# A gated linear attention decay in a four-branch decoder layer: other buffers, other place

## The chip, the cores and the metric

The kernel runs on one core of one Trainium2 chip. TensorE does the matrix products, VectorE, ScalarE and GpSimd the elementwise work, and SP (SyncE) issues all DMA transfers. The metric is the device time of one execution in microseconds (us), lower is better.

## The reference

One decoder layer over 2048 tokens of width 1024, all in float32. After an RMSNorm, one combined projection feeds four branches: A is RG-LRU, B an mLSTM, C is HGRN2, D is a gated linear attention (GLA). Each branch is gated by a SiLU path and projected, the four are merged by sigmoid gates, and one output projection, a residual and a last RMSNorm follow. C and D use the same chunked recurrence (chunks may be of another length, as long as the sums agree):

```python
log_gk = jax.nn.log_sigmoid(g_lr @ g_w_lr2 + g_b_lr2) / GLA_GATE_TAU      # tau 16, rank 16 -> 256 channels
og = gla_chunkwise(q, k, v, log_gk)
# gla_chunkwise, per chunk, with G the running sum of log_gk:
A = einsum(qc, kc, exp(G_t - G_s))            # s <= t
o = A @ vc + (qc * exp(G)) @ state
state = exp(G_last) * state + (kc * exp(G_last - G)).T @ vc
```

`g_lr` is the 16-wide, low-rank part of the combined projection. The decay `log_gk` of branch D is what the change is about.

## The kernel before, in words

The tokens are done in two halves of 1024. Each half goes through the same stages: the normalised input is split into a high and a low part (`hh`, `hl`, eight tiles each), because a float32 product is made of three products of rounded parts. Then most of the combined projection is done in pairs (`ahead_pairs`), its results going out to DRAM. Then come the mixers (`mixers`), the merge (`merge`) and the output projection (`outp`).

In `mixers` three things run beside each other. First, twelve tiles of 512 tokens, steps 0 to 11: steps 0 to 7 are HGRN2 heads, 8 to 11 are pairs of GLA heads. Each is one call of `gla_tile`. A tile clips the decay to a slot `g8` on GpSimd (L969), sums it up, forms the diagonal products (L993), then makes four sweeps over block sizes 8, 16, 32 and 64, each with its own temporary `w` (L1006) that GpSimd fills (L1012, L1013); at the end it transposes, scales by its gate (L1103) and sends the result to the array `y` in DRAM (L1106). Second, the mLSTM, whose pieces are traced between those of the tiles. Third, direct projections that fill TensorE: four value projections `ip_vals` (L280) and six late merge gates (`gates_ahead`, L268). Their weights are loaded by SP (L248), split by ScalarE (L249) and GpSimd (L250).

The last two value projections, at steps 4 and 6, also give 8 channels each of the low-rank input, which VectorE copies to `lrt` (L1125). `gla_decay` needs both. Per half it transposes `lrt` in two groups of four (L1168) and copies each group to a temporary `lt` (L1169); then, for two channel tiles and two token tiles, it multiplies by the 16-row weight `wlr` (L1175), adds the bias and applies Abs, Exp and Ln on ScalarE (L1177 to L1179 and, for Ln, the helper's L227) and ends with two operations on VectorE (L1181, L1182). Its four results are the decays of steps 8 to 11.

Temporaries come from an arena of 40 slots of 516 floats (the first 16 named `arena` in the trace, 8 `ma`, 16 `mb`). The arena hands out the next free slot in turn, at tracing time; what writes to a slot has to wait for the last use by the slot's owner before. PSUM has eight banks: two, `pb`, are taken in turn by the direct projections, six, `mx`, in turn by everything else in the mixers. A bank's or slot's users follow each other in the order in which they were traced.

The order of instructions on each engine is made by a list scheduler with its own timing model: what is ready goes by priority, and the priority is the place in the traced program, put forward by 4000 for the mixers (`mix`) and by 6000 for loads and evictions of projections. Engines run their queues in order. `lw` is a 128x1024 float tile that holds the LRU's weights earlier in each half and serves as a gate buffer in the merge. `merge` reads `y` back into `hh` and `hl` (L1291 to L1293), which it can only do when the direct projections have read these.

Of the kernel before, what the change touches and what calls it, by code (L numbers as in the profile page):

```python
# [8 lines left out]
F32 = mybir.dt.float32  # L9
# [6 lines left out]
P = 128  # L16
# [82 lines left out]
class Arena:  # L99


    def __init__(self, tile, n):
        self.where = [(tile, i) for i in range(n)]
        self.used = [False] * n
        self.live, self.at, self.peak = {}, {}, 0
        self.base, self.lim = 0, None
# [41 lines left out]
class Trunk:  # L148
    def __init__(self, ctx, tc, a, out, dbg=None):
        self.tc, self.nc, self.a, self.out, self.dbg = tc, tc.nc, a, out, dbg or {}  # L150
        nc = self.nc
        self.const = ctx.enter_context(tc.tile_pool(name="const", bufs=1))
        self.psum = ctx.enter_context(tc.tile_pool(name="psum", bufs=1, space=bass.MemoryType.PSUM))
        self.dram = ctx.enter_context(tc.tile_pool(name="dram", bufs=1, space=bass.MemoryType.DRAM))
        c = self.const
        self.hh = [c.tile([P, HT], F32R, name=f"hh{k}") for k in range(KT)]
        self.hl = [c.tile([P, HT], F32R, name=f"hl{k}") for k in range(KT)]
        self.wr = [c.tile([P, 528], F32, name=f"wr{k}") for k in range(3)]
        self.wh = [c.tile([P, 528], F32R, name=f"wh{k}") for k in range(NW)]
        self.wl = [c.tile([P, 528], F32R, name=f"wl{k}") for k in range(NW)]  # L160
        self.wi = self.gt = 0
        self.gth = [c.tile([P, 512], F32, name=f"gth{k}") for k in range(2)]
        self.ar = Arena(c.tile([P, NU * U], F32, name="arena"), NU)
        self.pb = [self.psum.tile([P, 512], F32, name=f"pb{i}") for i in range(NPB)]
        self.bi = 0
        self.tanhs, self.table = [], None
        self.mx = [self.psum.tile([P, 512], F32, name=f"mx{i}") for i in range(8 - NPB)]
        self.mi = 0
        self.ydram = [self.dram.tile([4, P, HT], F32, name=f"y{n}") for n in range(4)]
        self.gdram = [self.dram.tile([P, HT], F32, name=f"g{j}") for j in range(32)]  # L170
        self.pdram = {n: self.dram.tile([w, P, HT], F32, name=f"p{n}") for n, w in PRE + (("xm", 4), ("hf", 4), ("hg", 4))}
        self.mdram = [self.dram.tile([8, P, HT], F32, name=f"m{n}") for n in range(2)]
        self.adram = [self.dram.tile([P, 512], F32, name=f"a{k}") for k in range(4)]
        self.rdram = [self.dram.tile([2, 4, 512], F32, name=f"rdram{i}") for i in range(2)]
# [984 lines left out]
    def gla_decay(self):  # L1159

        nc = self.nc
        V, A, T = nc.vector, nc.scalar, nc.tensor
        gs = []
        lt = self.F()
        for n in range(2):
            ps = self.bank()
            for c in range(4):
                T.transpose(ps[0:16, c * 128:(c + 1) * 128], self.lrt[:, n * 4 + c, :], self.cs("id"))  # L1168
            V.tensor_copy(lt[0:16, n * 512:(n + 1) * 512], ps[0:16])  # L1169
        for p in range(2):  # L1170
            gs.append([self.T(0, NU + 2 * NA if p else None) for _ in range(2)])
            for n in range(2):
                g, t = gs[p][n], self.T()
                ps = self.bank()
                T.matmul(ps, self.wlr[:, p * 128:(p + 1) * 128], lt[0:16, n * 512:(n + 1) * 512], start=True, stop=True)  # L1175
                gg, tt = g[:, :512], t[:, :512]
                A.activation(gg, ps, AF.Identity, bias=self.pv("gb", p))  # L1177
                A.activation(tt, gg, AF.Abs)
                A.activation(tt, tt, AF.Exp, scale=-1.0)  # L1179
                self.ln(tt, tt, bias=1.0)  # L1180
                V.scalar_tensor_tensor(gg, gg, 0.0, tt, op0=ALU.min, op1=ALU.subtract)  # L1181
                V.tensor_scalar(gg, gg, 1.0 / 16, None, op0=ALU.mult)  # L1182
                self.free(t)
        self.free(lt)
        return gs


    def mixers(self):
        mix = lambda: self.prio(self.MIX)
        self.ahead = 0  # L1190
        low = NU + 2 * NA
        fill = iter(FILL)
        self.gates_ahead(next(fill))
        other = self.mlstm()
        due = 0.0

        def both(gen):

            nonlocal due
            for _ in iter(lambda: next(gen, 1), 1):  # L1200
                due += RATE
                while due >= 1:
                    due -= 1
                    next(other, None)

        with mix():
            for _ in range(LEAD):
                next(other, None)
        hv = self.ip_vals(0, 256)
        steps = [(j, gi) for j in range(6) for gi in range(2)]  # L1210
        gv, gd, loads = [], [], {}

        def load(s):
            j, gi = steps[s]
            if s >= LIM:
                self.ar.base, self.ar.lim = NTH, low
            if j < 4:
                loads[s] = [self.load_p(n, j, gi) for n in ("hq", "hf", "hg")], [self.load_p("hz", j, gi)]
            else:
                loads[s] = ([self.load_p(n, j - 4, gi) for n in ("gq", "gk")],  # L1220
                            [self.load_p("gz", 2 * j - 8 + i, gi) for i in range(2)])

        load(0)
        for s, (j, gi) in enumerate(steps):
            if s == 1:
                hv += self.ip_vals(1, 256)
            elif s == 4:
                gv += self.ip_vals(2, 264, self.lrt[:, :, 0:8])
            elif s == 6:
                self.ar.lim = low  # L1230
                gv += self.ip_vals(3, 264, self.lrt[:, :, 8:16])
                self.ar.lim = None
            elif s == 7:
                with mix():
                    gd = self.gla_decay()
            if s + 1 < len(steps):
                load(s + 1)
            self.gates_ahead(next(fill))
            x, zs = loads.pop(s)
            with mix():  # L1240
                if j < 4:
                    both(self.gla_tile(2, gi, [j], *x, [hv[j][gi]], zs, [(0, 128)], self.S[j], self.eps_h))
                else:
                    p = j - 4
                    both(self.gla_tile(3, gi, [2 * p, 2 * p + 1], *x, gd[p][gi], [v[gi] for v in gv[2 * p:2 * p + 2]], zs,
                                       [(0, 64), (64, 64)], self.S[j], self.eps_g))
        with mix():
            for _ in other:
                pass
        self.ar.base, self.ar.lim = 0, None  # L1250
# [298 lines left out]
```

## Time and profile before

| | |
|---|---|
| median of 3 runs | 2726.04 us (2724.26 to 2729.91) |
| the profiled execution | 2737.6 us |
| its span, first to last instruction | 2735.8 us |
| mean granted TensorE clock, as a share of 2.4 GHz | 0.977 |
| mixers, first half | about 740 to 1200 us, the last part beside the merge |
| mixers, second half | about 2100 to 2550 us, the last part beside the merge |
| decay, first half | 978.8 us (first transpose) to 1019 us |
| decay, second half | 2327.7 us to 2371 us |

A profile comes from one execution, so sums are made against its own time. In the rows, a busy share is an engine's share of the stretch, PEclk the granted clock as a share of full speed, and the text in brackets at the end of a timeline row says how long the engine sat idle before the instruction and which instruction's end released it. A matmul of float32 operands is recorded as two instructions.

### The profile page before, as it was taken

Reading aid. Unit: us, or ns where it says so; the run is one execution under the profiler, and the core shown is the slowest. Engines: PE = TensorE matmul, PEld = TensorE weight load, DVE = VectorE, ACT = ScalarE, POOL = GpSimd, SP = SyncE. Lnnn points to the kernel's source line nnn. Section 1 sums busy time; section 2 is a strip of 40 time slices with the busy share of each in tenths; the row PEclk is TensorE's granted clock in tenths of the full one; section 3 lists DMA queues with packets and bytes.
Section 4 is the critical chain, followed back from the end, with each engine's and each line's share of the span. In section 5 each row is a group of like instructions: output and inputs, shape, how many; then the busy total and the mean of one; then the engine's idle time right before and its main releaser. Section 6 shows DMA issues by size and latency. Waiting matters only on the chain. (4 is left out here: it accounts for less than half of the span.)

```text
span 2735.8 us, 45795 instructions
## 1 busy us (share of the span) xinstructions
PE 2604.2 (95%) x16800; PEld 2155.0 (79%) x16800; DVE 1739.0 (64%) x2907; ACT 1296.8 (47%) x2769; POOL 1500.4 (55%) x1273
## 2 busy tenths in 40 slices
PE   7999999999998898999999999999999999999999
PEld 5777878878788886778977777788787888776789
DVE  8787676447667778634376957754657667775332
ACT  5455444434444464452454454454345455644533
POOL 5566556444555555466475566554445555654753
PEclk9999999999999998999999999999999989999999
DMA  6233223443454336785442432243346433558721
GB/s 227 70 127 104 85 85 131 135 135 112 156 178 126 103 123 205 271 288 160 140 139 77 140 115 85 89 131 124 123 131 203 129 106 120 183 168 289 260 95 74
DMA packets 227073, 393.03 MB, mean 144 GB/s; under 512 B 20721, under 2 KB 78081, under 8 KB 226849
## 3 DMA queue, kind: packets, MB, share of 16 engines
q1 hardware_dynamic: 226848, 390.11, 43.2%
q8 instruction: 132, 2.16, 0.3%
q14 instruction: 93, 0.75, 0.1%
HBM read 270.42 MB, written 119.60 MB: 143 GB/s over the span
## 5 line engine op out<-in xcount | busy, mean ns | idle before, releaser
L418 POOL TENSOR_TENSOR wl<-wr,wh 128x512 fp32r<-128x512 f32 x264 | 370.2, 1407 | 300.5 <-ACT wh L417 292.2
L418 POOL TENSOR_TENSOR wl<-gth,wh 128x512 fp32r<-128x512 f32 x198 | 286.4, 1447 | 280.7 <-ACT wh L417 266.7
L423 PE MATMUL mx<-s,wh 128*128 128x512 f32 x1248 | 395.0, 396 | 5.5 <-DVE arena L432 2.4
L432 DVE TENSOR_TENSOR arena<-arena,mx 128x512 f32<-128x512 f32 x386 | 252.8, 681 | 184.4 <-PE mx L423 168.1
L250 POOL TENSOR_TENSOR wl<-wr,wh 128x512 fp32r<-128x512 f32 (+1 forms) x176 | 248.5, 1420 | 194.1 <-ACT wh L249 159.3
L423 PE MATMUL mx<-hh,wl 128*128 128x512 f32 x824 | 328.1, 398 | 9.4 <-POOL wl L418 9.4
L423 PE MATMUL mx<-hh,wh 128*128 128x512 f32 x824 | 326.8, 397 | 5.8 <-DVE mqk L624 3.6
L423 PE MATMUL mx<-hl,wh 128*128 128x512 f32 x824 | 327.5, 397 | 2.4 <-DVE hl L306 2.3
L268 PE MATMUL pb<-hh,wh 128*128 128x512 f32 x704 | 291.0, 415 | 11.4 <-DVE lw L1319 4.0
L268 PE MATMUL pb<-hl,wh 128*128 128x512 f32 x704 | 287.6, 409 | 3.2 <-DVE hl L1293 3.2
L268 PE MATMUL pb<-hh,wl 128*128 128x512 f32 x704 | 286.5, 407 | 0.0
L423 PEld LDWEIGHTS mx<-s,wh 128*128 128x128 f32 x1248 | 235.7, 189 | 62.7 <-DVE arena L432 2.8
L417 ACT ACTIVATE wh<-wr 128x512 fp32r<-128x512 f32 x264 | 164.2, 627 | 229.0 <-PE mx L423 142.6
L280 PE MATMUL pb<-wh,hh 128*128 128x256 f32 (+1 forms) x880 | 254.2, 290 | 3.6 <-DVE lrt L1125 2.3
L280 PE MATMUL pb<-wl,hh 128*128 128x256 f32 (+1 forms) x880 | 253.9, 289 | 1.7 <-POOL wl L250 1.7
L280 PE MATMUL pb<-wh,hl 128*128 128x256 f32 (+1 forms) x880 | 253.5, 288 | 0.0
L423 PE MATMUL mx<-s,wl 128*128 128x512 f32 x624 | 245.5, 397 | 0.0
L417 ACT ACTIVATE wh<-gth 128x512 fp32r<-128x512 f32 x198 | 124.3, 628 | 228.5 <-DVE gth L428 184.4
L423 PEld LDWEIGHTS mx<-hh,wl 128*128 128x128 f32 x824 | 155.8, 189 | 51.5 <-POOL wl L418 16.0
L423 PEld LDWEIGHTS mx<-hh,wh 128*128 128x128 f32 x824 | 156.4, 190 | 46.3 <-issue 7.0
L249 ACT ACTIVATE wh<-wr 128x512 fp32r<-128x512 f32 (+1 forms) x176 | 110.2, 629 | 165.0 <-PE pb L268 110.1
L423 PEld LDWEIGHTS mx<-hl,wh 128*128 128x128 f32 x824 | 155.9, 189 | 41.1 <-DVE hl L306 3.6
(614 smaller groups left out, 6081.8 us busy)
## 6 DMA issues: line engine op xcount, KB each, us to landing
wr<-in_wc_dram SPq DMA_DIRECT2D x246, 256.0 KB, 2.7
g<-arena SPq DMA_DIRECT2D x52, 512.0 KB, 3.4
gth<-in_wc_dram SPq DMA_DIRECT2D x66, 256.0 KB, 2.8
wr<-in_wb_dram SPq DMA_DIRECT2D x64, 256.0 KB, 3.3
hl<-y SPq DMA_DIRECT2D x32, 512.0 KB, 5.9
arena<-g SPq DMA_DIRECT2D x48, 256.0 KB, 4.5
arena<-in_xT_dram SPq DMA_DIRECT2D x32, 256.0 KB, 5.2
lw<-g SPq DMA_DIRECT2D x32, 256.0 KB, 3.6
```

Source lines behind the costliest of these rows:

```text
L249: nc.scalar.activation(hi, raw, AF.Copy)
L250: nc.gpsimd.tensor_tensor(lo, raw, hi, op=ALU.subtract)
L268: nc.tensor.matmul(ps, w[:, ws], h[:, ts], start=(k == 0 and i == 0), stop=(k == nk - 1 and i == 2))
L280: self.nc.tensor.matmul(v, h[:, cs], w[:, ws], start=(first and i == 0), stop=(last and i == 2))
L417: A.activation(hi, w, AF.Copy)
L418: G.tensor_tensor(lo, w, hi, op=ALU.subtract)
L423: nc.tensor.matmul(ps, wp[:, ws], xp, start=(k == 0 and i == 0), stop=(k == 3 and i == 2))
L432: V.tensor_tensor(o, x, y, op=ALU.add)
```

## The change

The transposed low-rank input goes to `lw` and no longer to an arena pair. The elementwise temporary of the four rounds is one tile of its own, `dt`, and no longer a new arena slot for each. The transposes and the 16-row matmuls take their banks from the direct projections' two, and no longer from the six others. The call stands in step 6, right behind the last value projection and ahead of that step's loads and tile, and no longer in step 7. To make room for `dt`, the scratch memory for DMA descriptors is made smaller. The rotation of both sets of banks is the same after the call as before, as six uses are a multiple of two and of six.

```diff
+        self.dt = c.tile([P, 512], F32, name="dt")
...
-        lt = self.F()
+        lt = self.lw.rearrange("p a b -> p (a b)")
         for n in range(2):
-            ps = self.bank()
+            ps = self.pbank()
...
-                g, t = gs[p][n], self.T()
-                ps = self.bank()
+                g = gs[p][n]
+                ps = self.pbank()
...
-                gg, tt = g[:, :512], t[:, :512]
+                gg, tt = g[:, :512], self.dt
...
-                self.free(t)
-        self.free(lt)
...
                 gv += self.ip_vals(3, 264, self.lrt[:, :, 8:16])
                 self.ar.lim = None
-            elif s == 7:
                 with mix():
                     gd = self.gla_decay()
...
-    nc = bacc.Bacc("TRN2", target_bir_lowering=False, num_devices=1)
+    nc = bacc.Bacc("TRN2", target_bir_lowering=False, num_devices=1, dynamic_dma_scratch_size=1024)
```

## Rows read from the trace of the kernel before

**Rows 1.** The page, busy time of each engine over the span.
```profile
PE 2604.2 (95%) x16800; PEld 2155.0 (79%) x16800; DVE 1739.0 (64%) x2907; ACT 1296.8 (47%) x2769; POOL 1500.4 (55%) x1273
```
**Rows 2.** The chain of waits, its longest piece: start, us, engine, tile, line.
```profile
2551.89 73.10 PE pb L268 x315
```
**Rows 3.** Table by stretches: busy PE, PEld, DVE, ACT, POOL; PEclk; DMA share; GB/s.
```profile
1000.00:1012.00 12.00, 12.00 (x77) 8.53 (x76) 5.73 (x14) 8.23 (x15) 4.58 (x6) 0.86 0.66 219
1028.00:1060.00 32.00, 24.09 (x324) 18.52 (x321) 31.49 (x52) 17.45 (x35) 16.62 (x17) 0.84 0.70 244
1084.00:1096.00 12.00, 11.08 (x134) 8.93 (x135) 9.18 (x21) 2.99 (x6) 5.56 (x6) 0.57 0.57 185
1084.00:1200.00 116.00, 109.94 (x1061) 84.77 (x1062) 62.40 (x118) 53.74 (x144) 51.48 (x52) 0.96 0.79 273
2352.00:2360.00 8.00, 8.00 (x42) 4.83 (x36) 3.46 (x7) 6.26 (x12) 2.80 (x4) 0.79 0.66 199
2376.00:2404.00 28.00, 21.82 (x256) 17.53 (x255) 27.47 (x43) 16.15 (x33) 16.23 (x14) 0.82 0.82 282
2425.00:2552.00 127.00, 118.72 (x1152) 90.47 (x1151) 66.48 (x125) 60.21 (x154) 57.61 (x56) 0.95 0.75 256
```
**Rows 4.** Timeline of GpSimd, first half: sweeps of step 7, then step 8.
```profile
1001.16 0.62 POOL L1012 TENSOR_TENSOR arena<-mb 128x256 f32<-128x256 f32 x1 [0.63 <-DVE mb L1181]
...
1017.13 1.41 POOL L1012 TENSOR_TENSOR arena<-mb 128x256 f32<-128x256 f32 x1 [2.68 <-DVE arena L1181]
1021.05 0.80 POOL L1012 TENSOR_TENSOR arena<-mb 128x256 f32<-128x256 f32 x1
...
1034.55 1.51 POOL L1012 TENSOR_TENSOR arena<-mb 128x256 f32<-128x256 f32 x1 [2.52 <-DVE mb L968]
...
1042.11 0.79 POOL L1012 TENSOR_TENSOR arena<-mb 128x256 f32<-128x256 f32 x1
```
**Rows 5.** Timeline of VectorE, first half: two of the decay's four L1181.
```profile
1000.09 0.99 DVE L1181 SCALAR_TENSOR_TENSOR mb<-mb,arena 128x512 f32<-128x512 f32 x1
...
1016.37 0.68 DVE L1181 SCALAR_TENSOR_TENSOR arena<-arena 128x512 f32<-128x512 f32 x1
```
**Rows 6.** Timeline of GpSimd, second half: first and last sweep of step 7.
```profile
2350.45 0.86 POOL L1012 TENSOR_TENSOR arena<-mb 128x256 f32<-128x256 f32 x1 [0.63 <-DVE mb L1181]
...
2372.43 0.61 POOL L1012 TENSOR_TENSOR arena<-mb 128x256 f32<-128x256 f32 x1
```
**Rows 7.** The decay's lines over both halves: ns min/median/max, first and last start.
```profile
L1168 PE MATMUL mx<-cst,lrt x16: 270/272/277, 978.8 to 2346.8; 128*16 128x128 f32 x16
L1175 PE MATMUL mx<-mb,wlr x16: 587/588/891, 991.7 to 2358.2; 16*128 16x512 f32 x16
L1169 DVE COPY mb<-mx x4: 667/670/678, 982.7 to 2350.3; 16x512 f32<-16x512 f32 x4
L1177 ACT ACTIVATE arena<-mx,pvt x6: 669/682/687, 1004.1 to 2358.8; 128x512 f32<-128x512 f32 x6
```
**Rows 8.** Timelines of SP and GpSimd: `y` transfer of step 6, clip of step 7.
```profile
1001.71 0.32 SPq L1106 DMA_DIRECT2D y<-arena  x1
...
978.20 1.49 POOL L969 TENSOR_SCALAR mb<-arena 128x512 f32<-128x512 f32 x1 [2.35 <-issue]
```
**Rows 9.** Timelines of VectorE and TensorE around the end of the value projections.
```profile
986.66 0.16 DVE L1125 COPY lrt<-pb 128x8 f32<-128x8 f32 x1
...
989.44 0.47 PE L268 MATMUL pb<-hh,wh 128*128 128x512 f32 x1
...
995.84 0.27 PE L1168 MATMUL mx<-cst,lrt 128*16 128x128 f32 x1
...
999.42 0.68 DVE L1169 COPY mb<-mx 16x512 f32<-16x512 f32 x1
...
1002.95 1.98 PE L1175 MATMUL mx<-mb,wlr 16*128 16x512 f32 x4
```
**Rows 10.** Table by stretches, only instructions on the direct projections' banks.
```profile
989.00:1004.00 15.00, 11.08 (x43) 7.13 (x41) 0.36 (x2) 0.86 (x2) 1.00 0.67 223
```

## The prediction

> **What bounds the kernel now.** I read the page's busy line first: TensorE is busy for 95% of the span, VectorE for 64%, GpSimd for 55% [rows 1]. The chain of waits ends in one unbroken run of projection matmuls on TensorE; its longest piece lasts 73.10 us [rows 2]. So time can only come from two places: from moments when TensorE has nothing to do, and from moments when its clock is granted at less than full speed. The change removes no matmul. I therefore went to the table by stretches and looked at TensorE's busy time and clock in the mixers and in the merge that follows, where the decay's results are used.
>
> The stretch in which the decay runs loses little: TensorE is busy for all 12 us from 1000, with the clock granted at 0.86. The loss comes after it, where the last direct projections have run out and the merge cannot yet go at full rate. From 1028 to 1060 TensorE is busy for 24.09 of 32 us at a clock of 0.84: 7.9 us idle and, at 0.16 of 32, 5.1 us of clock, 13.0 together. In the second half the same place (2376 to 2404) loses 6.2 and 5.0, which is 11.2. VectorE is what is full there, 31.49 of 32 and 27.47 of 28. The tail in which GLA tiles run beside the merge loses 6.1 + 4.6 and 8.3 + 6.4, together 25.4 us in 243 [rows 3]. The changed code can touch these 24.2 and 25.4 us, not the 2604 of work.
>
> The timeline of GpSimd shows what the decay does to the mixers now. In step 7 (the eighth tile) the first operation of the four sweeps, L1012, starts at 1001.16, and at 1021.05 for the last: 19.9 us for four sweeps. Two of them are released by L1181 of the decay. In the next tile, with no decay about, the same four take 1034.55 to 1042.11, 7.6 us [rows 4]. VectorE's L1181 rows fit: one ends at 1001.08, one at 1017.05, and the sweeps follow 0.08 us later [rows 5]. The code says why: the decay's four temporaries `t` and the four sweep temporaries `w` get the same arena slots, one after the other. In the second half the four sweeps take 2350.45 to 2372.43, 22.0 us [rows 6]. So tile 7 is held by up to 12.3 and 14.4 us per half.
>
> **The change, part by part.**
>
> Work: nothing is added or removed. Per half there are still 8 transposes of 0.27 us, 8 matmul records of 0.588 us (two to a matmul), two copies of 0.67 us, four Identities of 0.68 us and their followers [rows 7]. The decay issues no DMA and nothing on GpSimd, so no transfer moves with it; it is traced ahead of the loads for step 7 and of tile 6, but passes nothing of SP's or GpSimd's queue except by the slots that it takes. The smaller DMA scratch costs nothing: every DMA listed on the page is issued by SP. `lw` is next written by the merge's gate loads, which come tens of microseconds later; cost nothing.
>
> Temporary `dt`: tile 7's sweeps no longer wait for L1181, a gain of up to 12.3 and 14.4 us of lead for the mixers. What is late next? I followed the slots by hand. With four decay outputs taken before tile 6 and no `t`, tile 7's clipped decay (L969) falls on the slot of tile 6's gate, which must first go out to `y`; that transfer is issued at 1001.71, while L969 now starts at 978.20 [rows 8]. From 1002 the front of tile 7 needs seven instructions of 0.7 to 1.5 us by the nearest rows, about 7 us, so its sweeps can be joined at 1009 at the earliest instead of 1021. I take a lead of 8 us per half, two thirds of the upper end; the lower end is none.
>
> What the lead is worth: nothing at its own place, where TensorE is full, but VectorE has 12 - 5.73 = 6.3 us free there (8 - 3.46 = 4.5 in the second half) which it lacks in the full stretch [rows 3]. If that much mixer work moves forward, the full stretch shortens by as much, at its own loss of 13.0/32 = 0.41 and 11.2/28 = 0.40 per us: 2.6 + 1.8 = 4.4 us. The tail shortens by the 8 us of lead twice: 16 of 243 us, with 25.4 us lost in them, 1.7 us. Ends: none, and all the 24.2 us of the two full stretches.
>
> One `dt` for four rounds makes the next Abs wait for the last L1181. Behind it on ScalarE stand weight splits and evictions, for which GpSimd's L250 and then the projections wait. By rows a round is three activations and one L1181, about 2.6 us, so four take some 10 us. That ends near 1002 (now the last L1181 starts past 1016 [rows 5]), and its first user, tile 8, starts later; cost nothing. If that cover fails, the four rounds' 10 us fall on tile 8.
>
> Bank pair `pb`: the next gate's first matmul is queued behind the decay's last use of its bank, with the mixers' matmuls behind it on TensorE and the gate's eviction, and later the merge, waiting for it. The chain starts when the last but one value group has been copied (986.66 + 0.16): four transposes 1.1, copy 0.67, matmul 1.18, Identity 0.68, matmul 1.18, Identity 0.68: 5.5 us, ending at 992.3. The gate now starts at 989.44 [rows 9], so it is 2.9 us late at best. Of 15 us there, instructions on `pb` take 11.08, 74% of TensorE [rows 10], so 2.1 us would be idle; but two of the decay's matmuls (2.4 us), which now displace projections, lie in the hole. I take 0.5 us per half, 1.0 in all. The upper end: the copy now starts 3.3 us after the transpose before it has ended (996.11 to 999.42 [rows 9]); three such delays, one for the copy and one for each Identity, make the hole 12.8 us, 9.5 us idle per half.
>
> Clock: four records of the 16-row matmul stand together at 1002.95 (1.98 us [rows 9]), and around them the clock is granted at a mean between its 1.2 and 2.4 GHz levels although TensorE counts as busy: 0.14 of 12 us, 1.7 us, and 0.21 of 8, 1.7 us, in the second half [rows 3]. On two banks with an Identity between they can't stand together. I take half of the 3.4 as gained, 1.7. Ends: 3.4 gained, or a new fall of the size of 1084 to 1096, 0.43 of 12, 5.2 us per half [rows 3].
>
> Here the Trainium skill speaks against the change. In TensorE: Matmul & The Clock Gate (section "A second HAM failure mode: psum-queue depth-cycling") it says that a kernel which walks through PSUM banks in each iteration leaves TensorE idle for short moments so often that its clock falls back and forth. By that rule two banks for six uses would bring a new fall instead of ending one, and the sum would be on the slow side; the stretch from 1084 shows that the clock can be at 0.57 with TensorE busy for 11.08 of 12 us [rows 3].
>
> **Sum.** Against the profiled execution of 2737.6 us (span 2735.8 and 1.8 around it): -4.4 - 1.7 - 1.7 + 1.0 = -6.8, so 2730.8. The median of the runs shown is 2726.04, 0.99578 of that; the forecast on that scale is 2719.3 us, 0.25% faster.
>
> **Rivals.**
>
> No change: the lead is real and worth nothing, because TensorE's work is fixed and the merge's own copies of `y` through VectorE set the full stretch. For it: TensorE's 95%; and tile 7's new wait for the `y` transfer may eat the lead. Against it: VectorE is full exactly there. Time: 2737.6 - 1.7 + 1.0 = 2736.9, or 2725.3. If the change doesn't do what it says (the stall moves from the sweeps to L969), this is also the time.
>
> Slower: the two-bank chain starves TensorE behind the last value projection. For it: in-order queues on VectorE and ScalarE that delayed the decay's copy by 3.3 us; the projections have no other bank. Against it: the mixers' matmuls and the decay's own fill a quarter of the hole and more. With two delays the hole is 2.9 + 6.6 = 9.5 us, 7.0 idle per half, 14.0 in all; with the lead's 6.1 kept, +7.9: 2745.5, or 2733.9. With one fall of the clock, 5.2 more: 2739.1. It decides once more than 3.9 us per half are idle there, half of the 7.8 gained elsewhere.
>
> Much faster: both full stretches lose their idle time and their low clock: -24.2 - 1.7 + 1.0, or 2701. For it: VectorE's 100% there; against it, ten us of lead can't empty a stretch of 32.
>
> **How the numbers follow.** A measurement of this kernel can tell about 0.2%, 5.5 us, from no change. Forecast 0.40 (its own range 2712 to 2720), much faster 0.06, no change 0.28, slower 0.26. So faster 0.46, same 0.28, slower 0.26. The range runs from 2704, a third of the way from the far case's 2701 to the forecast's own low end, to 2737, most of the slow case.
>
> **What would show it.** Right: tile 7's four L1012 within some 8 to 12 us and none released by L1181; the 16-row matmuls apart; TensorE's idle time in the full stretches down from 7.9 and 6.2 us by 2 to 3 each. The gate's first matmul at most 3 us behind the last value matmul. L969 of tile 7 released by the `y` transfer shows my slot reading right. Wrong: more than 4 us of TensorE idle between the last value projection and the next gate, waiting on an L1177 or the copy; a clock under 0.8 there; or sweeps that are fast while the full stretches lose the same 24 us.

## The result: 1.2% slower, and the profile after

The changed kernel takes 2760.46 us in the median of 4 runs (2756.88 to 2761.73), the kernel before 2726.82 in the median of 4 (2724.26 to 2729.91): a ratio of 1.0121, 95% interval 1.0103 to 1.0138. The profiled execution took 2761.7 us with a span of 2759.9 us and a mean granted clock of 0.975. The forecast was 2719.3 us, the range 2704 to 2737.

Line numbers of the changed kernel are higher by one up to the decay (L1013 is L1012 of before, L971 is L970, L1104 is L1103), and lower by two in the merge.

The page's busy line after, in the columns of [rows 1], and the longest piece of the chain, as in [rows 2]:

```profile
PE 2613.9 (95%) x16800; PEld 2158.8 (78%) x16800; DVE 1723.6 (62%) x2907; ACT 1302.6 (47%) x2775; POOL 1499.8 (54%) x1273
```
```profile
2685.69 62.46 PE pb L281 x528
```

TensorE is busy for 9.7 us more and idle for 146.0 us (2759.9 - 2613.9), against 131.6 before. Its work is the same: busy time times mean clock is 2549 us after and 2544 before. So the 24.1 us between the two spans are 14.4 us more idle time and 9.7 us of the same work at a lower clock. The profiled execution of before is one of its slower ones (2737.6 against the median 2726.82), so this pair shows 24.1 of the 33.6 us between the medians. Two profiles below, scratch_only and empty_shift, have the instruction order of before; they show 131.3 and 125.3 us idle, and spans of 2723.6 and 2729.4 us. One profile can thus differ from another by 12 us; a verdict goes by the medians.

ScalarE has six instructions more (2775 against 2769, [rows 1]). In the traces all six are loads of its function tables, 41 in place of 35, 7.7 us of its time. So the new order did add work, which the prediction had put at none. It can't be the whole cost: lw_only below has 29 such loads and is slower than before too.

The table by stretches, from the first second scan (L970) of a half's mixers to the first output eviction, before and then after; the third row of before is for further down. Columns as in [rows 3].

```profile
742.00:1307.00 565.00, 521.80 (x4816) 444.76 (x4815) 357.22 (x740) 265.80 (x719) 316.45 (x308) 0.97 0.57 185
2092.00:2659.00 567.00, 531.30 (x4819) 452.54 (x4818) 354.29 (x739) 269.74 (x721) 318.50 (x307) 0.95 0.54 175
...
968.00:1000.00 32.00, 32.00 (x278) 28.73 (x276) 22.10 (x59) 18.02 (x59) 14.26 (x14) 1.00 0.33 108
```
```profile
742.00:1324.00 582.00, 533.24 (x4810) 451.38 (x4809) 347.72 (x739) 270.51 (x723) 316.27 (x308) 0.95 0.55 180
2107.00:2683.00 576.00, 530.97 (x4816) 450.38 (x4815) 351.25 (x739) 271.29 (x723) 314.65 (x307) 0.96 0.53 173
```

The two stages are 17 and 9 us longer; what lies between and behind them is within 2 us of before (785 and 77 us before, 783 and 77 after). The stretches of [rows 3] after, with two more ahead of them, where the last value projections run:

```profile
968.00:1000.00 32.00, 24.79 (x261) 20.80 (x261) 19.13 (x54) 17.16 (x45) 16.29 (x20) 0.87 0.31 99
...
976.00:984.00 8.00, 5.92 (x67) 5.88 (x68) 5.21 (x16) 2.15 (x5) 3.63 (x5) 0.66 0.01 2
1000.00:1012.00 12.00, 12.00 (x66) 8.64 (x65) 7.41 (x20) 8.67 (x26) 3.67 (x5) 0.92 0.20 68
1028.00:1060.00 32.00, 27.61 (x271) 22.15 (x258) 26.75 (x42) 18.30 (x38) 22.28 (x20) 0.95 0.84 287
1084.00:1200.00 116.00, 108.82 (x1150) 83.58 (x1149) 62.93 (x119) 52.52 (x142) 55.35 (x58) 0.94 0.67 231
2352.00:2360.00 8.00, 7.77 (x43) 5.09 (x42) 6.13 (x18) 5.72 (x11) 2.62 (x4) 1.00 0.66 217
2376.00:2404.00 28.00, 24.55 (x173) 19.78 (x172) 23.48 (x37) 16.43 (x39) 17.70 (x13) 0.88 0.63 208
2425.00:2552.00 127.00, 116.25 (x1195) 88.97 (x1194) 67.72 (x129) 52.61 (x142) 54.30 (x57) 0.96 0.63 220
```

The two full stretches lose less than before: 4.4 + 1.6 us (idle time, and one minus the clock times the length) from 1028, against 13.0, and 3.5 + 3.4 from 2376, against 11.2. But these are fixed times, and what happens there has moved. Right behind the first one, from 1060 to 1070, 6.0 us are now lost and none before. The mixers of the second half start 15 us later than before, and 15 us later the full stretch loses 8.7 us:

```profile
1060.00:1070.00 10.00, 7.30 (x92) 5.28 (x91) 8.92 (x15) 0.86 (x4) 1.25 (x1) 0.67 0.63 187
2391.00:2419.00 28.00, 24.33 (x223) 19.90 (x224) 26.70 (x42) 17.48 (x36) 15.55 (x16) 0.82 0.86 301
```

From 968 to 1000 TensorE now idles for 7.2 us, with a clock of 0.87 and for 8 us of 0.66; before, it was busy for all 32 us at full clock. And the tails lose more: 7.2 us idle from 1084 and 10.8 from 2425, against 6.1 and 8.3.

The two longest of these holes, 4.7 us, stand in the middle of the last value projection, before the decay takes a bank. TensorE's queue has come to the diagonal products of step 6 (L994), whose input is late. By the profile, ScalarE's Exp for them (L975) waits for a result that has to go out to `y` first:

```profile
973.46 0.63 ACT L975 ACTIVATE mb<-mb 128x512 f32<-128x512 f32 x1 [3.56 <-DMA y<-mb]
```
```profile
974.87 0.65 PE L994 MATMUL mx<-mb,mb 128*32 128x32 f32 x32 [2.12 <-DVE mb L977]
978.08 0.66 PE L994 MATMUL mx<-mb 128*32 128x32 f32 x32 [2.56 <-DVE mb L1017]
```

GpSimd after, first half: the clip of step 6, the four sweeps of step 7, the clip of step 7.

```profile
963.84 1.53 POOL L970 TENSOR_SCALAR mb<-arena 128x512 f32<-128x512 f32 x1 [2.68 <-DMA y<-mb]
...
995.97 0.61 POOL L1013 TENSOR_TENSOR mb<-arena 128x256 f32<-128x256 f32 x1
...
1002.97 0.61 POOL L1013 TENSOR_TENSOR mb<-arena 128x256 f32<-128x256 f32 x1 [5.77 <-DVE arena L945]
...
1004.15 0.62 POOL L1013 TENSOR_TENSOR mb<-arena 128x256 f32<-128x256 f32 x1
...
1013.57 0.61 POOL L1013 TENSOR_TENSOR mb<-arena 128x256 f32<-128x256 f32 x1 [4.30 <-PE mx L1103]
...
1016.76 1.55 POOL L970 TENSOR_SCALAR arena<-mb 128x512 f32<-128x512 f32 x1
```
and SP's issue of step 6's result to `y`:
```profile
1014.25 0.32 SPq L1107 DMA_DIRECT2D y<-arena  x1
```

No sweep of step 7 waits for the decay any more, and the last of the four starts 7.5 us earlier than before (1021.05 [rows 4]). But the clip of step 6 waits for a transfer of an mLSTM result out of the slot that it took over. Step 7's, as read by hand, has to wait for that of step 6; its row shows no wait, as GpSimd had other work until then, but in own_decays below, which takes no slots for the decay, it comes at 986.41. Here it comes at 1016.76, against 978.20 [rows 8], now behind its own sweeps; the tile's end moves from 1046.59 (L1103) to 1068.04 us.

The last value matmul, the decay's first transposes, its 16-row matmuls and the first matmul of the next gate, after:

```profile
989.42 0.29 PE L281 MATMUL pb<-wh,hl 128*128 128x264 f32 x1
...
989.98 0.60 PE L1169 MATMUL pb<-cst,lrt 128*16 128x128 f32 x4
991.35 1.12 PE L1176 MATMUL pb<-lw,wlr 16*128 16x512 f32 x2 [0.77 <-DVE lw L1170]
...
995.28 1.12 PE L1176 MATMUL pb<-lw,wlr 16*128 16x512 f32 x2
...
1001.62 1.27 PE L1176 MATMUL pb<-lw,wlr 16*128 16x512 f32 x2
...
1004.39 0.48 PE L269 MATMUL pb<-hh,wh 128*128 128x512 f32 x1
...
1007.57 1.12 PE L1176 MATMUL pb<-lw,wlr 16*128 16x512 f32 x2
```

The call stands earlier in the program, but the decay does not run earlier: its first transposes come at 989.98, before at 978.81 [rows 7], and the last round's L1182 at 1018.36, before (L1181) at 1018.48. The next gate starts 14.7 us behind the last value matmul, 9.9 in the second half. These two holes, in the table by stretches:

```profile
989.71:1004.39 14.68, 12.30 (x75) 8.24 (x73) 10.09 (x26) 9.33 (x30) 7.75 (x10) 0.88 0.59 190
2349.07:2358.92 9.85, 8.85 (x61) 5.22 (x59) 7.02 (x19) 7.16 (x18) 5.42 (x6) 1.00 0.80 260
```

### The profile page after: what moved, and what is told of

It is laid out like the page before. It is cut to its first block, busy times and chain, and to the rows that moved or that the text cites. A ratio compares the mean times of both kernels' runs of the same rounds, so it can differ in the third digit from the quotient of the medians.

```text
span 2759.9 us, 45783 instructions
## 1 busy us (share of the span) xinstructions
PE 2613.9 (95%) x16800; PEld 2158.8 (78%) x16800; DVE 1723.6 (62%) x2907; ACT 1302.6 (47%) x2775; POOL 1499.8 (54%) x1273
## 3 DMA queue, kind: packets, MB, share of 16 engines
q1 hardware_dynamic: 226848, 390.11, 42.9%
## 5 line engine op out<-in xcount | busy, mean ns | idle before, releaser
L424 PEld LDWEIGHTS mx<-hh,wl 128*128 128x128 f32 x824 | 156.0, 189 | 51.4 <-POOL wl L419 15.8
```

The lines of the kernel that those rows point to most:

```text
L424: nc.tensor.matmul(ps, wp[:, ws], xp, start=(k == 0 and i == 0), stop=(k == 3 and i == 2))
```

## The experiments

Each verdict is a ratio to runs of the kernel before on the same chip. The last columns are single profiles: idle time of TensorE over the span, the clock, and what is lost (idle time plus one minus the clock, times the length) in two stretches of each half, first half / second half. "Head" is 200 to 260 us behind the stage's first second scan, where the last value projections run; "tail" is from 400 us behind it to the first output eviction. The first three rows are profiles of one order of instructions; they differ by up to 4.9 us in a head and 3.3 in a tail, so a smaller difference between two profiles can't be read.

| kernel | ratio (95%) | idle | clock | head | tail |
|---|---|---|---|---|---|
| before | 1 | 131.6 | 0.977 | 4.5 / 5.1 | 4.1 / 10.1 |
| scratch_only | 0.9990 (0.9974 to 1.0007) | 131.3 | 0.982 | 4.2 / 3.3 | 0.8 / 11.4 |
| empty_shift | 1.0011 (0.9992 to 1.0030) | 125.3 | 0.978 | 9.1 / 6.5 | 1.4 / 8.8 |
| the change | 1.0121 (1.0103 to 1.0138) | 146.0 | 0.975 | 15.8 / 7.9 | 15.2 / 13.4 |
| own_decays | 1.0120 (1.0091 to 1.0149) | 146.8 | 0.974 | 15.9 / 13.1 | 6.5 / 11.9 |
| slots_only | 1.0084 (1.0054 to 1.0114) | 134.0 | 0.979 | 6.1 / 6.7 | 12.6 / 14.7 |
| six_banks | 1.0117 (1.0089 to 1.0145) | 151.4 | 0.974 | 2.1 / 1.8 | 39.8 / 31.2 |
| step7 | 1.0109 (1.0078 to 1.0140) | 150.9 | 0.974 | 7.2 / 3.6 | 13.1 / 17.3 |
| own_buffers_only | 1.0052 (1.0035 to 1.0068) | 142.5 | 0.979 | 5.6 / 3.3 | 8.9 / 12.1 |
| own_buffers_padded | 1.0047 (1.0029 to 1.0065) | 136.9 | 0.979 | 6.3 / 3.5 | 3.6 / 10.2 |
| lw_only | 1.0050 (1.0032 to 1.0068) | 134.3 | 0.974 | 4.1 / 5.5 | 8.0 / 17.1 |
| dt_only | 1.0116 (1.0081 to 1.0150) | 146.3 | 0.974 | 4.1 / 4.5 | 18.5 / 12.4 |
| banks_only | 1.0063 (1.0047 to 1.0078) | 133.6 | 0.974 | 7.3 / 6.6 | 6.0 / 5.9 |
| place_only | 1.0265 (1.0250 to 1.0281) | 179.5 | 0.963 | 3.6 / 1.9 | 54.8 / 49.3 |
| after_step8_slots | 1.0139 (1.0107 to 1.0172) | 152.3 | 0.973 | 11.9 / 8.0 | 23.0 / 16.0 |
| shift_two_slots | 1.0063 (1.0044 to 1.0081) | 141.0 | 0.977 | 5.8 / 3.8 | 8.9 / 12.1 |
| shift_six_slots | 1.0030 (1.0017 to 1.0044) | 134.5 | 0.977 | 7.6 / 5.6 | 3.7 / 8.7 |
| order_only | 1.0046 (1.0025 to 1.0067) | 133.8 | 0.975 | 4.0 / 3.5 | 8.0 / 13.7 |
| after_own_early | 1.0179 (1.0163 to 1.0195) | 150.0 | 0.971 | 12.6 / 7.5 | 19.2 / 17.8 |
| before_own_early | 1.0060 (1.0045 to 1.0075) | 138.1 | 0.975 | 4.2 / 5.7 | 14.4 / 2.2 |

**Undo one part.** First theories: S, the decay's four results hold arena slots through step 6, so tiles 6 and 7 start late; B, the two direct banks; P, the place. (In the expectations T stands for own buffers: `dt`, `lw` and the scratch.)

own_decays, the changed kernel with the four results in tiles of their own:
```diff
+        self.gdt = [c.tile([P, 512], F32, name=f"gd{i}") for i in range(4)]
...
-            gs.append([self.T(0, NU + 2 * NA if p else None) for _ in range(2)])
+            gs.append(self.gdt[2 * p:2 * p + 2])
```


> The change as it is, but the four decay results get four tiles of their own and no arena slots, so steps 6 and 7 are given the slots they would have without them. Theory S (slots): the loss comes from the clip of step 6 waiting for an mLSTM transfer to y and that of step 7 waiting for step 6's; without it the second scan of step 6 starts near 946 us again and that of step 7 near 980, and the kernel takes 2710 to 2730 us. Theory B (banks): the projections stop behind the last value projection because the decay holds their two banks; that stays, so 2750 to 2765 us. Theory P (place): being traced ahead of steps 6 and 7 makes the decay's work push theirs aside; also 2750 to 2765.

slots_only, own buffers with the call in step 7 on six banks, but the four result slots taken in step 6:
```diff
-            gs.append([self.T(0, NU + 2 * NA if p else None) for _ in range(2)])
+            gs.append(self.gslots[p])
...
+                self.gslots = [[self.T(0, NU + 2 * NA if p else None) for _ in range(2)] for p in range(2)]
+            elif s == 7:
```


> The decay stands in step 7 again and uses the six banks again, but its four result slots are taken in step 6, so every tile from step 6 on has the same arena slots as with the change. The own temporary and lw stay. Theory S: as slow as the change, 2750 to 2765 us, with the scans of steps 6 and 7 near 965 and 1018. Theories B and P: as before or a little faster, 2715 to 2730.

six_banks, the changed kernel on the six banks:
```diff
-            ps = self.pbank()
+            ps = self.bank()
...
-                ps = self.pbank()
+                ps = self.bank()
```


> The change with the decay's transposes and matmuls on the six banks again. Theory S: still 2750 to 2765 us. Theory B: 2715 to 2735, and TensorE's idle time between 990 and 1000 us (1.6 us of 8) goes. Theory P: 2750 to 2765.

step7, the changed kernel with the call back in step 7:
```diff
                 self.ar.lim = None
+            elif s == 7:
                 with mix():
                     gd = self.gla_decay()
```


> The change with the call in step 7 again, on the two banks and with the own temporary. The result slots are then taken after step 6. Theory S: step 6 is free again (scan near 946), step 7's clip falls on a slot whose owner, an mLSTM gate, goes out to y near 1000, so step 7 is still about 20 us late: 2735 to 2750 us. Theory B: still 2750 to 2765. Theory P: 2715 to 2730.

With own_decays step 6's second scan is back at 946.01 us (965.40 after, 945.96 before) and the tail loses less, yet the median stays: S alone falls. So do B and P as single causes. The head does tell something. All four kernels that have both the early place and the two banks lose 11.9 us or more there in the first half and 7.5 or more in the second; all others 9.1 or less, and 6.7 or less. The steps between the two groups, 2.8 and 0.8 us, are within what one order's profiles differ by; only that the ranks agree in both halves speaks for it. What is squeezed out is seen in the busy time on the direct banks `pb` in one 60 us stretch, columns PE, PEld, DVE, ACT, clock, DMA: before, after, and six_banks.

```profile
942.00:1002.00 60.00, 36.97 (x221) 30.29 (x222) 2.78 (x16) 2.65 (x9) 1.00 0.40 125
```
```profile
942.00:1002.00 60.00, 30.24 (x189) 24.92 (x189) 4.11 (x18) 3.40 (x10) 0.91 0.35 111
```
```profile
942.00:1002.00 60.00, 42.08 (x245) 35.27 (x245) 2.80 (x16) 3.25 (x10) 1.00 0.37 113
```

In the change TensorE gets through 6.7 us less on `pb` than before, though the decay's own matmuls are in that count. Its longest holes there come from step 6, as shown. In own_decays step 6 is on time, and the loss sits where the decay holds the two banks, from the last value matmul to the next gate, first and second half:

```profile
992.10:1010.63 18.53, 12.29 (x71) 5.71 (x70) 14.36 (x26) 12.58 (x40) 10.66 (x10) 0.63 0.41 126
2350.85:2374.52 23.67, 17.33 (x136) 9.30 (x136) 20.99 (x44) 14.42 (x38) 12.96 (x12) 0.60 0.47 150
```

That is 6.2 and 6.3 us idle, of which 1.9 and 3.5 wait for VectorE's copy of the transposes, and with the clock 13.1 and 15.8 us lost, 28.9 in all, where this kernel is 33 us slower by the medians. In the change the same two holes lose 4.1 and 1.0 us. So own_decays is as slow as the change, but loses its time in another place: without the waits on slots, the two banks cost more. On six banks TensorE gets through 5.1 us more than before on `pb` and loses nearly nothing there, but then tile 7's second scan comes at 1030.42 (979.72 before) and the tail loses 39.8 us: the loss moved, and the time stayed.

**One part alone.** Theory D: the smaller scratch. Theory O: the own buffers by themselves. Theory R: any edit here shifts the scheduler's order and the slots of all that follows, and that costs.

scratch_only:
```diff
-    nc = bacc.Bacc("TRN2", target_bir_lowering=False, num_devices=1)
+    nc = bacc.Bacc("TRN2", target_bir_lowering=False, num_devices=1, dynamic_dma_scratch_size=1024)
```


> The kernel before with the one edit that all four slower experiments share with the change and that I had put at nothing: the smaller scratch memory for DMA descriptors. Its instruction order is that of the kernel before on every engine. Theory D (the smaller scratch costs, all over the run): 1.008 to 1.012, 2749 to 2760 us. Theory O (what costs is the temporary dt and the buffer lw themselves: four rounds in series on one tile) and theory R (any edit here shifts the order that the list scheduler makes and the rotation of the arena's slots for all that follows, and that pattern, not one wait, costs): 1.000, 2726 us.

own_buffers_only, the changed kernel with both edits, that of six_banks and that of step7:


> Of the change only dt, lw and the scratch; the call in step 7 and on the six banks, as before. Six slots fewer are taken in step 7, so steps 8 to 11 get others than before. Prediction's own sum: 8 us per half off the sweeps of step 7, 2719 us. Theories D, O and R all say slow: 1.006 to 1.012, 2742 to 2760 us. Were it 1.000 or faster, the four slow runs would have come each from its own part, place or banks.

own_buffers_padded, the same with the old slots taken and given back unused:
```diff
+        pad = self.F()
...
+                g, t = gs[p][n], self.T()
```


> As own_buffers_only, but the pair and the four slots that the decay used before are taken and given back at the same points without being used, so every tile has the arena slots of the kernel before. Theory O: as own_buffers_only, within 5 us of it. Theory R with the slots as the carrier: within 0.3% of before, 2719 to 2734 us. Theory R with the order as the carrier: anything between.

empty_shift:
```diff
             elif s == 7:
+                self.free(*[self.T() for _ in range(1)])
```


> The kernel before with one arena slot taken and given back at once ahead of the decay in step 7: no instruction is added, removed or changed, the decay keeps its own buffers, place, banks and scratch; only the slots handed out after it are other ones, and with them the scheduler's order. Theories D and O: 1.000, 2720 to 2733 us. Theory R: slower, 1.004 to 1.012, 2736 to 2760 us.

D falls. Own buffers cost half a per cent with either slots. The empty shift was no shift: the decay's pair starts on an even slot, which swallowed it, and the order was that of before; it only shows how well a ratio repeats.

lw_only and dt_only split the own buffers, banks_only and place_only make one edit each to the kernel before. In this order:
```diff
-        lt = self.F()
+        lt = self.lw.rearrange("p a b -> p (a b)")
...
-        self.free(lt)
```


> The kernel before with one edit of the change: the transposed low-rank input goes to lw. The four arena temporaries, the place, the banks and the scratch stay. Own buffers together cost 1.0052. Theory W (lw: the merge's first two gate loads, at 207.87 and 368.25 us before, can only go behind the decay, and its order shifts): 1.004 to 1.006, 2737 to 2746 us. Theory C (the one dt, which puts the four rounds in series and ends the decay 12 us later): 1.000, 2722 to 2735 us.


```diff
+        self.dt = c.tile([P, 512], F32, name="dt")
...
-                g, t = gs[p][n], self.T()
+                g = gs[p][n]
...
-                gg, tt = g[:, :512], t[:, :512]
+                gg, tt = g[:, :512], self.dt
...
-                self.free(t)
```


> The kernel before with the other half: the four rounds share dt (with the smaller scratch that it needs, which costs nothing, 0.999), lt stays an arena pair. Theory C: 1.004 to 1.006, 2737 to 2746 us, with the decay's last L1182 near 1031 us in place of 1019. Theory W: 1.000, 2722 to 2735 us.


```diff
-            ps = self.bank()
+            ps = self.pbank()
...
-                ps = self.bank()
+                ps = self.pbank()
```


> The kernel before with the banks alone: the decay's six uses go to the two direct banks, in step 7, with its own four arena temporaries. With dt and lw the banks added 0.6% (1.0109 against 1.0052). Theory A (each part has its own price, which adds): 1.005 to 1.007, 2740 to 2748 us. Theory I (the banks cost only because each round on the one dt keeps a direct bank until ScalarE comes to it): 1.000 to 1.002.


```diff
                 self.ar.lim = None
-            elif s == 7:
                 with mix():
```


> The kernel before with the place alone: the call in step 6 ahead of its tile, with arena buffers and six banks. Ten slots are taken there, so step 6's tile finds still fewer free than in the change, and its clip and that of step 7 wait for a y transfer as in slots_only (second scans near 965 and 1015 us). With dt and lw the place added 0.65% (1.0117 against 1.0052), the slots alone 0.3% (1.0084). Theory A: 1.003 to 1.008, 2735 to 2750 us. Theory I (the place is harmless where the rounds have four temporaries): 1.000 or faster, 2710 to 2727 us.

Every part alone is slower, and they don't add: 0.5 + 1.2 + 0.6 + 2.7 is 5.0%, the change 1.2%. `dt` alone ends the decay later, as theory C said (its last L1182 at 1033.27 us; before, as L1181, at 1018.48), and costs 1.2%; with `lw` beside it only 0.5%. Why is not settled. In place_only the expected scans near 965 and 1015 us did not come (951.23 and 954.17); there step 7's first difference `d` (L973) stands 88.4 and 89.7 us behind its second scan, 12.8 and 14.2 before, which is the longest such gap in any of these kernels.

**Shifts without a change, and a gap.** Theory M came from the traces: in the change the first difference `d` of step 9 (L974) stands 42.9 us behind the second scan that feeds it. VectorE's scan, TensorE's last product with a value of step 8, and GpSimd's `d`, which took that value's slot:

```profile
1045.92 1.21 DVE L971 TENSOR_TENSOR_SCAN ma<-cst,ma 128x512 f32<-128x512 f32 x1
```
```profile
1088.24 0.49 PE L1080 MATMUL mx<-ma,mb 128*128 128x128 f32 x2
```
```profile
1088.81 1.04 POOL L974 TENSOR_TENSOR ma<-ma 128x512 f32<-128x512 f32 x1 [8.39 <-PE mx L1080]
```

after_step8_slots:
```diff
             x, zs = loads.pop(s)
+            if s == 8:
+                self.ar.at[False] = 33
```


> The changed kernel with one assignment more: ahead of step 8's tile the arena's next slot is set to 33, so that step 8's sweeps take low slots again and step 9's first difference d (L974) falls on a slot that step 8 gives back early, no longer on the value tile that step 8 reads last. In the changed kernel d came 42.9 and 40.6 us after the second scan of step 9, before 1.3 and 2.2. Theory M (this wait carries the loss that the place adds to own buffers): the gap falls under 15 us and the time to 1.003 to 1.007, 2734 to 2746 us. Theory R (no single wait; any shift of slots and order costs): the gap falls too, but the time stays at 1.009 to 1.013, 2750 to 2762 us.

shift_two_slots and shift_six_slots (the line of empty_shift with `range(2)` and `range(6)`):


> The kernel before with two arena slots taken and given back at once ahead of the decay in step 7; no instruction is added, removed or moved in the traced program (with one slot, as in empty_shift, the pair's alignment swallowed the shift and the order was that of before). Step 9's d now falls on the slot pair at of step 8, which step 8 reads to its end. Theory M: a gap of 25 to 45 us at step 9 and 1.005 to 1.012, 2740 to 2760 us. Theory that only the change's own instructions cost: 1.000, 2722 to 2736 us.

> As shift_two_slots with six slots, the number that the change takes less. Step 9's d falls on a decay of step 8, which is read early. Theory M: no gap over 15 us at d, within 0.3% of before, 2720 to 2737 us. Theory R: as any other shift, 1.004 to 1.012, 2738 to 2760 us.

order_only:
```diff
             elif s == 7:
-                with mix():
+                with self.prio(self.MIX + 300):
```


> The kernel before with the decay's priority put forward by 4300 in place of 4000: same slots, banks, buffers and traced order, only the scheduler's order changes (135 of VectorE's instructions stand elsewhere, against 423 in the change). Theory M: no gap, 1.000 to 1.002, 2722 to 2736 us. Theory R with the order as the carrier: 1.003 to 1.008.

The gap left step 9 (1.3 us) and came back at step 10, there waiting for a result that has to go out to `y` first:

```profile
1099.99 1.22 DVE L971 TENSOR_TENSOR_SCAN arena<-cst,arena 128x512 f32<-128x512 f32 x1 [1.61 <-POOL arena L970]
```
```profile
1140.14 1.04 POOL L974 TENSOR_TENSOR arena<-arena 128x512 f32<-128x512 f32 x1 [7.81 <-DMA y<-arena]
```

The two shifts and the other order, which change no line of work in the program, cost 0.3 to 0.6%, each with an interval above 1. ScalarE's table loads are 33 and 41 in the shifts; order_only keeps the 35 of before and is the cleanest of the three, 0.46%. M's gap of 25 us or more in shift_two_slots did not come (7.6 at most from step 7 on); the kernel was slower without it.

after_own_early and before_own_early, the early temporaries of steps 8 to 11 in tiles of their own:
```diff
+        self.eo = [c.tile([P, 512], F32, name=f"eo{k}") for k in range(4)]
...
+        pg, own = g8, n == 3
+        if own:
+            g8 = self.eo[0]
...
-        d, wq, wk = self.T(), self.T(), self.T()
+        pd = d, wq, wk = self.T(), self.T(), self.T()
+        if own:
+            d, wq, wk = self.eo[1:]
```


> The changed kernel, where the four early temporaries g8, d, wq and wk of the GLA steps 8 to 11 are tiles of their own, shared by the four steps; the arena slots that they had are still taken and given back, so all else has the slots of the changed kernel. No early temporary can then wait for the step before to end. The gap between second scan and d (42.9 and 40.6 us at step 9) should fall under 15 us at every step from 8 on, in both halves. Theory M (the gap carries what the change costs beyond the 0.3 to 0.6% that any shift costs): 1.003 to 1.007, 2737 to 2748 us. Theory R (shift alone): 1.009 to 1.013, 2753 to 2765 us.

> The same four tiles in the kernel before (with the smaller scratch that they need, which costs nothing). There the gap is 1.3 to 7.6 us at steps 8 to 11, so there is nothing to take away; a control of what the tiles do by themselves. Theory M: 1.000 to 1.006, 2729 to 2746 us, as any shift. A time below 0.998 would mean that the early temporaries' slots hold the kernel before back too.

M falls: the gap at step 9 is 4.3 and 12.4 us, a later one comes up (39.8 at step 11), and the kernel is slower still. own_decays also has the gap at step 9 (48.2 and 49.4 us), and its last tile ends earlier than before. A tile that may begin early is no gain in itself. Step 10, second scan and end, before, then in after_own_early, where it starts 67 us earlier and ends 37 us later:

```profile
1090.42 1.45 DVE L970 TENSOR_TENSOR_SCAN arena<-cst,arena 128x512 f32<-128x512 f32 x1
...
1152.61 0.69 DVE L1103 TENSOR_TENSOR arena<-mx,arena 128x512 f32<-128x512 f32 x1 [0.78 <-PE mx L1102]
```
```profile
1023.24 1.23 DVE L975 TENSOR_TENSOR_SCAN eo<-cst,eo 128x512 f32<-128x512 f32 x1 [0.56 <-POOL eo L974]
...
1190.07 0.69 DVE L1110 TENSOR_TENSOR arena<-mx,arena 128x512 f32<-128x512 f32 x1 [0.46 <-PE mx L1109]
```

What goes with the time better than any one wait is the end of the last tile, first half, before and after:

```profile
1199.32 0.69 DVE L1103 TENSOR_TENSOR arena<-mx,arena 128x512 f32<-128x512 f32 x1 [2.37 <-PE mx L1102]
```
```profile
1226.70 0.69 DVE L1104 TENSOR_TENSOR arena<-mx,arena 128x512 f32<-128x512 f32 x1 [0.86 <-PE mx L1103]
```

This operation starts 457 and 460 us behind the stage's first second scan (first and second half), and in the change 485 and 484 us. In six kernels it starts 475 us or more behind it in both halves: the change, six_banks, dt_only, place_only, after_step8_slots and after_own_early. They are six of the seven slowest, 1.0116 to 1.0265. The seventh, own_decays, has it at 449 and 447, earlier than before, and loses its time in the head. That is a pattern in single profiles; no run tests it by itself.

No kernel here beats the one before.

## Why the prediction was wrong

**The lead of tile 7** (-4.4 and -1.7) is the step that failed. Its first half was right: no sweep is released by the decay, and the last of the four starts 7.5 us earlier, near the 8 that I took. But I took this lead of the sweeps for a lead of the tile. The tile's clip and diagonal products, which I had ahead of the sweeps, came behind them, and the tile ends 21.5 us later. I had seen that its clip would wait for step 6's `y` transfer, but reckoned it from the old time of that transfer, 1001.71; it is issued at 1014.25, as step 6 had itself slipped by 19 us behind a clip on an mLSTM slot, which I had not followed. The second half of the step, that a lead passes on to the end of the stage, also failed: the last tile starts its last operation 27 and 24 us later in the stage, and the early starts of after_own_early end late. Where the last tile did end earlier, by 8 and 13 us in own_decays, the kernel is as slow. The no-change rival had named the sign that came, the stall moving from the sweeps to L969, but put its time at 2725.3.

**What the full stretches are worth.** At their fixed times they lost 7.0 and 4.4 us less than before, more than the 2.6 and 1.8 of the sum, but that does not hold in the stage's own time. Between head and tail, 260 to 400 us behind the first second scan, 17.9 us are lost after 22.8 in the first half and 24.3 after 17.4 in the second, so together 2.0 us more. The rest of the loss came in the head, 11.3 and 2.8 us more, and in the tail, 11.1 and 3.3 more, by the table.

**The bank chain** (+1.0) was mis-sized. The hole from the last value matmul to the next gate is 14.7 us in the first half and 9.9 in the second, not 2.9. For the copy itself TensorE waits 0.77 us in the first half. The hole is filled mostly by matmuls of the mixers and of the decay: 2.4 and 1.0 us of it are idle, 3.4 in place of 1.0, with 1.8 us of clock more in the first half. That is under the 3.9 per half at which the slower rival was to decide. So the time came out on the slow side without that rival's starving in the change; of the 10.4 us idle in the first head, 4.7 are step 6's. In own_decays the rival is seen in full, 6.2 and 6.3 us idle and a clock of 0.63 and 0.60. The banks are not the whole either: six_banks takes the head's loss away and is not faster.

**The clock at the 16-row matmuls** (-1.7) came true at its place: they stand apart, and the clock from 1000 to 1012 is 0.92 after 0.86, from 2352 to 2360 1.00 after 0.79: 12 x 0.06 and 8 x 0.21, 2.4 us. But from 990 to 1000, where two of them stand now, it is 0.93 after 1.00, and from 976 to 984, far from them, 0.66. The mean clock of the span did not rise (0.975 after 0.977). The Trainium skill's rule in TensorE: Matmul & The Clock Gate (section "A second HAM failure mode: psum-queue depth-cycling") speaks of such falls for kernels that walk through banks and leave TensorE idle for short moments. In the two holes of own_decays, where TensorE idles between uses of the two banks, the trace agrees: the clock is 0.63 and 0.60 there. Over the whole kernel the runs show no difference between six banks and two, 0.974 with six_banks and 0.975 in the change.

**Costs put at nothing.** The scratch: right, 0.9990. `lw`: 1.0050, which can't be told from the 1.003 to 1.006 of a bare shift. `dt`: wrong, 1.0116 alone; there it ended the decay 15 us later. In the change, too, the four rounds that I put at 10 us, ending near 1002, take 19.2 us from the first L1182 (999.19) to the last, so the decay ends no earlier than before. The place, "passes nothing of SP's or GpSimd's queue except by the slots that it takes": 1.0265 alone, where it takes ten of the 40 slots in step 6. That exception had no term. In the change it carries a part, the late tiles 6 and 7; how much of the time is not shown, as own_decays takes no such slots and is as slow.

**What the sum lacked** is the term for everything behind the edit. Each number was worked out on the old order of instructions, and the order and the slots of steps 6 to 11 were made anew. Of VectorE's 2907 instructions 503 stand outside the longest sequence that the traces of before and after share, 153 in order_only. Shown is that all three such reshuffles that were run cost 0.3 to 0.6% with no other edit. Whether others would be faster was not tried, nor whether the order of before is a lucky one among many. Shown too are a head that loses 11.3 us more in the first half, in part by step 6's slots and in part by the banks, and tails that lose 12.6 us or more in the first half in all six kernels that take arena slots for the decay in step 6, though also in three that do not. What brings the rest of the 1.2% in each kernel is open; undoing one part moved the loss and did not lower it. Six banks and own result tiles together, which would take both carriers of the head's loss away, were not run.

## What to carry to other kernels

Where a scheduler fixes the order ahead and buffers rotate, price an edit first by a control that shifts slots or priorities and changes nothing else: here it cost 0.3 to 0.6%, more than the forecast's gain of 0.25%. When a buffer is taken earlier, follow who gets its slot next and when that slot's last reader or transfer ends, for several steps, with the new times and not the old. A wait removed from one tile is worth nothing unless the last tile ends earlier, and own_decays shows that even this is not enough, as TensorE lost the time elsewhere. Compare stretches by their place in the stage, not by their time from the start of the run.

## What the runs showed that was not expected

Idle time often comes with a lower granted clock, so that a hole costs more than its length: from 1084 to 1200, after, 7.2 us idle stand beside a clock of 0.94 of 116 us, which is another 7.0 us, and in the first hole of own_decays 6.2 us idle stand beside 6.9 us of clock. It is no fixed price: the change's second hole has 1.0 us idle at a clock of 1.00, and over the span lw_only has the clock of six_banks, 0.974, with 17 us less idle time (134.3 against 151.4). And one program's profiles differ by 12.2 us in span (2735.8 and 2723.6) with the same order, idle time within 0.3 us and the clock 0.977 and 0.982: there it was the clock alone.
